# Turning the values of a gated delta rule: blocks on VectorE and a pass through DRAM in place of TensorE transposes

## The chip, the cores and the metric

The kernel runs on one core of one Trainium2 chip. The metric is device time in microseconds (us) of one execution; a kernel's time is the median of its runs.

## The reference

The reference is one inference step of a decoder layer with two parallel branches, a gated delta rule (A) and an indexer-sparse attention (B), for one prompt of 256 tokens and eight sequences of eight new tokens each. One wide input projection feeds both branches. Of branch A this matters here:

```python
h = rms_norm(x, pre_norm_g) * (1.0 + scale[:, None]) + shift[:, None]
(a_qkv, a_z, a_b, a_a, b_q, ...) = split_columns(h @ w_in)
...
qkv, conv_new = causal_short_conv(a_qkv, conv_buf, conv_w)
q, k, v = jnp.split(qkv, [A_QK, 2 * A_QK], axis=-1)
...
v = v.reshape(B, L, GDN_V_HEADS, GDN_DV)
...
o, s = gated_delta_rule(q, k, v, g, beta, s0)
```

There are 16 heads of q and k and 32 of v, all 128 wide. The delta rule needs each value head with tokens along one axis and the head's 128 channels along the other, while the projection delivers it with channels on the partitions.

## The kernel before, in words

All of the layer's large products are one stream on TensorE (`stream`). It takes blocks of 128 output columns of a weight matrix; each block is two units, one for each half of the 2048 input rows. A unit is 24 matmuls of 128x320 (256 prompt tokens and 64 new ones): weights are split in two parts (`whi` by ScalarE, `wlo` by VectorE as the difference), and the unit multiplies `whi` with `xh` and `xl`, then `wlo` with `xh`. The raw weights come in tiles `raw`, three tiles of two halves, so six units' worth; a half is 512 KB in rows of 512 bytes. `split_ahead` splits two units ahead of the one that is multiplied. The results of a block lie in a PSUM bank `pm`.

The recurrent stage (`gdn_chunks`) runs through eight groups of two q/k heads and four value heads. A group's blocks are k, q, z and v heads in this order. When a block is done, its function (`k_done`, `q_done`, `z_done`, `v_done`) takes it through a short convolution (`conv`); a value head ends in `vf`, a tile of 128 channels by 384 columns: 256 of the prompt, then for each sequence eight of the keys' and eight of the queries' places. After every second value head, `v_then` starts four generators for that pair of heads, h:

- `v_gen` turns the pair's values into `vt`, of 128 tokens by 3 blocks of tokens by 2 heads by 128 channels, and scales each token;
- `prompt_chain` and `sample_chain` do the recurrence, with `vt` and with `XT`, the inverse of a triangular matrix;
- `norm_gen` normalises, turns back and multiplies with z.

The inverse (`inverse`) is made once for a group, by GpSimd on 32x32 blocks; it stores `BT` to DRAM as 32x32 blocks (`d_b`), loads them as `blk`, and returns the result through `d_x`. Both chains wait for it and for `vt`.

The order on every engine is fixed when the program is built. The generators are advanced by `side_round`, twice in each unit. A planner, `Clock`, keeps an estimated time for each engine and for the DMA engines; a generator that yields a time is not advanced before TensorE's estimated time has reached it. For a transfer, `enter` charges each row with at least 512 bytes at 320 GB/s, and takes it to have landed 2.2 us after that. So a change of these costs moves instructions, though it changes none of them.

Nearly all transfers are issued by SyncE's queue in this fixed order: the weights, the states `S`, the buffers `cst` of the convolution, `gbt` with the decays, the stores of results. An issue stands at the head until what it waits for is there. `stream` and the planner issue a weight load when its half-tile is free, by the planner's time.

In `v_gen` before, each pair of heads takes two PSUM banks `ps`, `p` and `q`. TensorE turns the two heads' three blocks of 128 tokens in six 128x128 transposes (`self.tr`, a matmul with the identity `ident`), and ScalarE copies them to `vt` in three scalings by `sst`:

```python
for t in range(2):
    self.tr(p[:, 256 * t + 128 * v:256 * t + 128 * v + 128], vf[:, 128 * t:128 * t + 128])
self.tr(q[:, 128 * v:128 * v + 128], vf[:, 256:384])
```

There are two tiles `vt` and three `vf`. `vt` is free again when both chains of its pair are done.

Of the kernel before, what the change touches and what calls it, by code (L numbers as in the profile page):

```python
# [7 lines left out]
F32 = mybir.dt.float32  # L8
# [3 lines left out]
AF = mybir.ActivationFunctionType  # L12
# [38 lines left out]
class Engine:  # L51


    def __init__(self, engine, name, enter):
        self.engine, self.name, self.enter = engine, name, enter
# [11 lines left out]
class Engines:  # L67
    def __init__(self, nc, enter):
        for name in ("tensor", "vector", "scalar", "gpsimd", "sync"):
            setattr(self, name, Engine(getattr(nc, name), name, enter))  # L70


class Clock:
# [79 lines left out]
    def enter(self, name, op, args, kw):  # L153
        out = args[0] if args else kw["out"]
        rest = list(args[1:]) + list(kw.values())
        ins = [a for a in rest if hasattr(a, "tensor") and a is not out and a is not kw.get("accum_out")]
        outs = [out] + ([kw["accum_out"]] if kw.get("accum_out") is not None else [])
        if op == "transpose":
            ins = ins[:1]
        own = None if "dma" in op else name  # L160
        start = max(self.t[name], self.ready(*ins, name=own))
        if "dma" not in op or out.space != MEM.DRAM:
            start = max(start, self.idle(*outs, name=own))
        if name in ("vector", "scalar"):
            banks = {a.tensor.name for a in outs + ins if a.space == MEM.PSUM}
            for b in banks:
                start = max([start] + [t for e, t in self.bank.get(b, {}).items() if e != name])
        if "dma" in op:
            side = out if out.space != MEM.DRAM else ins[0]
            rows = self.free(side) // min(out.shape[-1], ins[0].shape[-1])  # L170
            size = side.shape[0] * rows * max(512, 4 * min(out.shape[-1], ins[0].shape[-1]))
            self.t[name] = start + (1.0 if name == "gpsimd" else 0.55)
            self.t["dma"] = max(self.t["dma"], start) + size / 3.2e5
            end = max(self.t["dma"], start) + 2.2
        else:
            if kw.get("op") == OP.pow or OP.pow in rest:
                took = 1.6
            else:
                took = self.cost(name, op, outs, ins)
            end = self.t[name] = start + took  # L180
            end += 0.2 if name == "tensor" else 0.1
        if name in ("vector", "scalar"):
            for b in banks:
                self.bank.setdefault(b, {})[name] = end
        by = "dma" if "dma" in op else name
        for a in ins:
            self.note(self.used, a, by, end)
        for a in outs:
            self.note(self.written, a, by, end)
        self.last = max(self.last, end)  # L190
# [11 lines left out]
class Kernel:  # L202
# [209 lines left out]
    def build(self):  # L412
        nc, tc = self.nc, self.tc
# [4 lines left out]
        f = self.fix  # L418
# [11 lines left out]
        self.d_z = self.dram.tile([32, 128, NT], F32, name="d_z")  # L430
        self.d_yb = self.dram.tile([KB, 128, NT], F32, name="d_yb")
        self.d_g = self.dram.tile([32, 384], F32, name="d_g")
        self.d_qi, self.d_q = (self.dram.tile([NB, 32, 4, 128], F32, name=n) for n in ("d_qi", "d_q"))
        self.d_b = [self.dram.tile([4, 12, 32, 32], F32, name=f"d_b{j}") for j in range(2)]
        self.d_x = [self.dram.tile([2, 4, 12, 32, 32], F32, name=f"d_x{j}") for j in range(2)]
# [2 lines left out]
        c = self.open("gdnc")  # L438
# [1553 lines left out]

    def v_gen(self, h, G):

        e, hv, K = h % 2, 2 * h, self.K[h]
        while "ready" not in G:
            yield
        yield self.ready(self.V[hv], self.V[hv + 1], G["sst"])
        yield from self.need(self.vt)
        yield from self.need(self.ps_side, 2)  # L2000
        vt = self.vt.get()
        p, q = self.psum(), self.psum()
        for v in range(2):
            vf = self.V.pop(hv + v)
            for t in range(2):
                self.tr(p[:, 256 * t + 128 * v:256 * t + 128 * v + 128], vf[:, 128 * t:128 * t + 128])
            self.tr(q[:, 128 * v:128 * v + 128], vf[:, 256:384])
            self.vf.put(vf)
        for t in range(3):
            src = p[:, 256 * t:256 * t + 256] if t < 2 else q[:, 0:256]  # L2010
            self.act(vt[:, t], src.rearrange("p (v d) -> p v d", v=2), AF.Copy,
                     scale=G["sst"][:, 20 + 3 * e + t:21 + 3 * e + t])
        self.ps_side.put(p)
        self.ps_side.put(q)
        K["vt"], K["users"] = vt, 2

    def drop_vt(self, K):
# [421 lines left out]
```

## Time and profile before

| What | us |
|---|---|
| Median of 3 runs | 2153.73 (2153.57 to 2154.71) |
| The profiled execution | 2151.39 |
| Its span, from the first to the last instruction | 2149.6 |
| TensorE matmuls busy | 2122.4 |
| VectorE busy | 1402.6 |
| ScalarE busy | 991.3 |
| GpSimd busy | 462.3 |

The profile is of one execution. Names stand without their buffer numbers: `ps<-ident,vf` is a matmul that writes a bank `ps` from `ident` and `vf`. PE is TensorE's matmuls and PEld its loads of weights, which overlap them; DVE is VectorE, ACT ScalarE, POOL GpSimd, SPq the queue of SyncE. In a group of instructions the figures are the busy time of all, the mean of one in ns, and the idle time of the engine just before them with what ended it. Nearly all instructions carry one line number, that of a helper that records them, so that groups are told apart by their tiles. The stage of the recurrence lies from about 730 to 1670 us; the value turns lie between 800 and 1560 us.

### The profile page before, as it was taken

What the parts mean: (1) busy time and instruction counts of PE and PEld (TensorE: products, weight loads), DVE (VectorE), ACT (ScalarE), POOL (GpSimd) and SP (SyncE); (2) the same over time, 40 slices, a digit from 0 to 9 for tenths busy, and PEclk for the clock granted to TensorE, in tenths of its full rate; (3) what the DMA queues carried; (4) which work ended last, traced back from release to release, by engine and by line L of the source; (5) the groups of instructions that cost most, each with busy time, mean ns of one, the idle gap of its engine ahead of it and who ended that gap; (6) DMA issues with size and microseconds to landing.
All of it is one profiled execution on the core that took longest, in us unless ns stands there. A gap on an engine that the chain in (4) does not pass through costs nothing.

```text
span 2149.6 us, 44001 instructions
## 1 busy us (share of the span) xinstructions
PE 2122.4 (99%) x17087; PEld 2028.8 (94%) x17087; DVE 1402.6 (65%) x2864; ACT 991.3 (46%) x2257; POOL 462.3 (22%) x645
## 2 busy tenths in 40 slices
PE   7999999999999999999999999999999999999997
PEld 6889999999999999899999999999999999999997
DVE  4665555889754577877777777777746645445443
ACT  3225465333343455465656565656545424323343
POOL 1001000000011018353535353536350000000000
PEclk9999999999999999999999999999999999999999
DMA  9995555985688766777777777777786967555562
GB/s 336 356 293 154 164 159 150 288 260 153 183 245 246 204 179 177 203 199 207 200 204 209 196 204 200 211 192 197 197 233 199 273 186 214 160 157 144 164 181 87
DMA packets 720336, 438.91 MB, mean 204 GB/s; under 512 B 74144, under 2 KB 705536, under 8 KB 717824
## 3 DMA queue, kind: packets, MB, share of 16 engines
q1 hardware_dynamic: 716032, 413.45, 68.2%
q0 software_dynamic: 3616, 21.02, 2.9%
q8 instruction: 134, 2.20, 0.4%
q10 hardware_dynamic: 480, 1.65, 0.2%
q14 instruction: 74, 0.61, 0.1%
HBM read 386.81 MB, written 48.94 MB: 203 GB/s over the span
## 4 chain that ended last, share of the span: by engine, by line
PE 71%; issue 23%; DMA 2%; DVE 2%; ACT 1%; SPq 0%; DVEq 0%; POOL 0%; POOLq 0%
PE pm L61 55%; PE ps L61 16%; DMA raw<-in_w_ada_dram 1%; DVE S L61 1%; DMA a<-in_w_ada_dram 1%; DVE ps L61 0%; DVE wlo L61 0%; SPq L61 0%; DMA c<-in_c_sample_dram 0%; DMA out_dram<-S 0%; ACT ot L61 0%; DMA cst<-in_state_conv_dram 0%; DVE w L61 0%; ACT whi L61 0%; DVE sc L61 0%
## 5 line engine op out<-in xcount | busy, mean ns | idle before, releaser
L61 PE MATMUL pm<-xh,whi 128*128 128x320 f32 x3284 | 1005.7, 319 | 0.6 <-ACT whi L61 0.3
L61 PE MATMUL pm<-xl,whi 128*128 128x320 f32 x3284 | 971.9, 309 | 0.3 <-DVE xl L61 0.3
L61 DVE TENSOR_TENSOR wlo<-raw,whi 128x1024 fp32r<-128x1024 f32 x474 | 587.4, 1248 | 291.7 <-ACT whi L61 270.3
L61 PEld LDWEIGHTS pm<-xh,whi 128*128 128x128 f32 x3284 | 617.1, 188 | 30.6 <-issue 24.4
L61 PEld LDWEIGHTS pm<-xl,whi 128*128 128x128 f32 x3284 | 617.6, 188 | 1.7 <-DVE xl L61 0.8
L61 ACT ACTIVATE whi<-raw 128x1024 fp32r<-128x1024 f32 x474 | 498.1, 1058 | 163.2 <-PE pm L61 149.9
L61 PE MATMUL pm<-xh,wlo 128*128 128x320 f32 x3284 | 553.3, 309 | 0.0
L61 PEld LDWEIGHTS pm<-xh,wlo 128*128 128x128 f32 x3284 | 499.3, 188 | 0.0
L61 POOL TENSOR_TENSOR X<-X,tmpx 48x31 f32<-48x31 f32 (+15 forms) x248 | 175.2, 706 | 19.4
L61 POOL TENSOR_TENSOR tmpx<-blk,X 48x31 f32<-48x31 f32 (+15 forms) x248 | 162.0, 653 | 52.1 <-DMA blk<-d_b 34.0
L61 PE MATMUL pm<-y1h,whi 128*128 128x320 f32 x512 | 151.3, 309 | 1.0 <-ACT y1h L61 1.0
L61 PE MATMUL pm<-y1l,whi 128*128 128x320 f32 x512 | 151.2, 308 | 0.1
L61 DVE SCALAR_TENSOR_TENSOR ps<-xp,cs,ps 128x344 f32<-128x344 f32 x192 | 111.5, 581 | 6.8
L61 POOL TENSOR_TENSOR rfin<-rfin,mh 128x3 f32<-128x3 f32 x1 | 0.8, 848 | 485.9 <-DVE rfin L61 485.9
L61 POOL TENSOR_TENSOR sc<-sc,mh 128x6 f32<-128x6 f32 (+1 forms) x24 | 43.5, 1814 | 280.7 <-DVE sc L61 253.8
L61 PEld LDWEIGHTS pm<-y1h,whi 128*128 128x128 f32 x512 | 96.2, 188 | 1.3 <-ACT y1h L61 1.3
L61 PEld LDWEIGHTS pm<-y1l,whi 128*128 128x128 f32 x512 | 95.9, 187 | 0.3 <-DVE y1l L61 0.3
L61 PE MATMUL pm<-y1h,wlo 128*128 128x320 f32 x512 | 85.4, 308 | 0.0
L61 PEld LDWEIGHTS pm<-y1h,wlo 128*128 128x128 f32 x512 | 77.7, 188 | 0.0
L61 DVE SCALAR_TENSOR_TENSOR S<-S,gtr,ps 128x128 f32<-128x128 f32 x256 | 67.5, 342 | 0.1
L61 ACT ACTIVATE xp<-pm 128x256 f32<-128x256 f32 (+1 forms) x128 | 32.0, 304 | 71.1 <-PE pm L61 71.1
L61 ACT ACTIVATE ot<-ot,sc 128x128 f32<-128x128 f32 x96 | 29.9, 390 | 71.8 <-DVE sc L61 71.8
(372 smaller groups left out, 2319.8 us busy)
## 6 DMA issues: line engine op xcount, KB each, us to landing
raw<-in_w_in_dram SPq DMA_DIRECT2D x336, 512.0 KB
raw<-in_w_pa_dram SPq DMA_DIRECT2D x64, 512.0 KB
rawx<-in_w_ada_dram SPq DMA_DIRECT2D x18, 1024.0 KB
a<-in_w_ada_dram SPq DMA_DIRECT2D x16, 1024.0 KB
S<-in_state_gdn_dram SPq DMA_DIRECT2D x32, 512.0 KB
out_dram<-S SPq DMA_DIRECT2D x32, 512.0 KB
raw<-in_w_pb_dram SPq DMA_DIRECT2D x32, 512.0 KB
raw<-in_w_out_dram SPq DMA_DIRECT2D x32, 512.0 KB
```

What stands on the lines that cost most here:

```text
L61: made = fn(*args, **kw)
```

## The change

`v_gen` no longer uses TensorE or PSUM. It takes `vt` as soon as a tile is free, without waiting for the scale factors `sst`. VectorE transposes each head's `vf` in blocks of 32x32 straight into half of `vt` (`nc.vector.transpose` on 128x384), which leaves every block turned within its own place but the blocks themselves in channel order. Eight transfers then store `vt` to a new DRAM tensor `d_v` of 384 tokens by 2 heads by 128 channels, one for each head and each group of 32 channels; each writes rows of 32 numbers, 128 bytes, to their token's place. A ninth transfer loads `d_v` into the same `vt`, now in token order, in rows of 1 KB. ScalarE scales `vt` in place, when the load is there and the factors are.

Beside that, the planner charges a transfer's row with at least 256 bytes instead of 512, for all transfers of the kernel.

```diff
-            size = side.shape[0] * rows * max(512, 4 * min(out.shape[-1], ins[0].shape[-1]))
+            size = side.shape[0] * rows * max(256, 4 * min(out.shape[-1], ins[0].shape[-1]))
...
+        self.d_v = [self.dram.tile([384, 2, 128], F32, name=f"d_v{j}") for j in range(2)]
...
     def v_gen(self, h, G):
 
+        nc = self.nc
         e, hv, K = h % 2, 2 * h, self.K[h]
+        yield self.ready(self.V[hv], self.V[hv + 1])
+        yield from self.need(self.vt)
+        vt = self.vt.get()
+        yield self.idle(vt)
+        blocks = vt.rearrange("p t v d -> p (t v d)")
+        for v in range(2):
+            vf = self.V.pop(hv + v)
+            self.emitted += 1
+            nc.vector.transpose(blocks[:, 384 * v:384 * v + 384], vf)
+            self.vf.put(vf)
+        yield
+        d = self.d_v[e]
+        for v in range(2):
+            for i in range(4):
+                src = blocks[32 * i:32 * i + 32, 384 * v:384 * v + 384]
+                nc.sync.dma_start(d[:, v, 32 * i:32 * i + 32].rearrange("(n r) c -> r n c", r=32),
+                                  src.rearrange("r (n c) -> r n c", c=32))
+        yield max(self.ready(d), self.idle(vt))
+        nc.sync.dma_start(vt, d.rearrange("(t p) v c -> p t v c", t=3))
         while "ready" not in G:
             yield
-        yield self.ready(self.V[hv], self.V[hv + 1], G["sst"])
-        yield from self.need(self.vt)
-        yield from self.need(self.ps_side, 2)
-        vt = self.vt.get()
-        p, q = self.psum(), self.psum()
-        for v in range(2):
-            vf = self.V.pop(hv + v)
-            for t in range(2):
-                self.tr(p[:, 256 * t + 128 * v:256 * t + 128 * v + 128], vf[:, 128 * t:128 * t + 128])
-            self.tr(q[:, 128 * v:128 * v + 128], vf[:, 256:384])
-            self.vf.put(vf)
+        yield self.ready(vt, G["sst"])
         for t in range(3):
-            src = p[:, 256 * t:256 * t + 256] if t < 2 else q[:, 0:256]
-            self.act(vt[:, t], src.rearrange("p (v d) -> p v d", v=2), AF.Copy,
-                     scale=G["sst"][:, 20 + 3 * e + t:21 + 3 * e + t])
-        self.ps_side.put(p)
-        self.ps_side.put(q)
+            self.act(vt[:, t], vt[:, t], AF.Copy, scale=G["sst"][:, 20 + 3 * e + t:21 + 3 * e + t])
         K["vt"], K["users"] = vt, 2
```

What it moves is seen in the lists of instructions as they stand in the two programs. On TensorE, at the first pair of value heads, before: the end of one unit (`whi`, then eight `wlo`), the six turns into the banks ps_69 and ps_70, and the next unit's first matmul.

```order
L61 MATMUL pm_66<-xh,whi_78 128x320
L61 MATMUL pm_66<-xl,whi_78 128x320
L61 MATMUL pm_66<-xh,wlo_81 128x320 x8
L61 MATMUL ps_69<-ident,vf_7336 128x128 x2
L61 MATMUL ps_70<-ident,vf_7336 128x128
L61 MATMUL ps_69<-ident,vf_7337 128x128 x2
L61 MATMUL ps_70<-ident,vf_7337 128x128
L61 MATMUL pm_65<-xh,whi_79 128x320
```

The same place now:

```order
L61 MATMUL pm_66<-xh,whi_78 128x320
L61 MATMUL pm_66<-xl,whi_78 128x320
L61 MATMUL pm_66<-xh,wlo_81 128x320 x8
L61 MATMUL pm_65<-xh,whi_79 128x320
L61 MATMUL pm_65<-xl,whi_79 128x320
```

The units follow each other directly. Over the whole program TensorE has 96 matmuls fewer and none more; some of the chains' pieces stand a little earlier or later among the units.

On SyncE's queue, where the third group begins, before: weight loads (raw), the recurrent states S, a result w, two z tiles zf and the decays gbt.

```order
L61 DMA out_dram<-w_7359 128x2x128
L61 DMA S_7366<-in_state_gdn_dram 128x8x128 x2
L61 DMA out_dram<-S_7367 128x8x128 x2
L61 DMA raw_75<-in_w_in_dram 128x8x128
L61 DMA out_dram<-w_7361 128x2x128
L61 DMA zf_7342<-d_z 128x320
L61 DMA zf_7340<-d_z 128x320
L61 DMA raw_75<-in_w_in_dram 128x8x128
L61 DMA gbt_7343<-d_g 128x768
L61 DMA raw_76<-in_w_in_dram 128x8x128
```

And now, at the place that answers to it:

```order
L61 DMA S_7368<-in_state_gdn_dram 128x8x128 x2
L61 DMA out_dram<-w_7363 128x2x128
L61 DMA out_dram<-S_7369 128x8x128 x2
L61 DMA raw_75<-in_w_in_dram 128x8x128
L61 DMA d_v_90<-vt_7357 32x12x32 x8
L61 DMA raw_75<-in_w_in_dram 128x8x128
L61 DMA zf_7344<-d_z 128x320
L61 DMA zf_7343<-d_z 128x320
L61 DMA gbt_7345<-d_g 128x768
L61 DMA raw_76<-in_w_in_dram 128x8x128
L61 DMA vt_7357<-d_v_90 128x3x256
```

The eight stores stand between two weight loads, and the load of `vt` comes two weight loads later. It is much the same at most of the other pairs.

On the same queue one group earlier, at the first pair of the second group, before:

```order
L61 DMA raw_77<-in_w_in_dram 128x8x128 x2
L61 DMA blk<-d_b_93 48x1024
L61 DMA raw_75<-in_w_in_dram 128x8x128
L61 DMA out_dram<-S_7366 128x8x128 x2
L61 DMA raw_75<-in_w_in_dram 128x8x128
L61 DMA out_dram<-w_7358 128x2x128
L61 DMA S_7366<-in_state_gdn_dram 128x8x128 x2
L61 DMA out_dram<-S_7367 128x8x128 x2
L61 DMA raw_76<-in_w_in_dram 128x8x128
L61 DMA cst_104<-in_state_conv_dram 24x256
```

And now:

```order
L61 DMA raw_75<-in_w_in_dram 128x8x128 x2
L61 DMA blk<-d_b_95 48x1024
L61 DMA out_dram<-S_7368 128x8x128 x2
L61 DMA S_7368<-in_state_gdn_dram 128x8x128 x2
L61 DMA out_dram<-w_7360 128x2x128
L61 DMA out_dram<-S_7369 128x8x128 x2
L61 DMA out_dram<-w_7363 128x2x128
L61 DMA d_v_90<-vt_7357 32x12x32 x8
L61 DMA cst_106<-in_state_conv_dram 24x256
```

Before, weight loads stand between the stores and loads of states. Now there is none from `blk` on, nor behind the last row: three more loads of `cst`, two of `S`, eight stores `out_dram<-cst` and one load of `gbt` follow before the next `raw`. These are 32 issues in a row; nowhere else in the stage are there so many.

## Prediction

> **What bounds the kernel now.** I read the page's head first: which engine is full, and over what span.
>
> ```profile
> span 2149.6 us, 44001 instructions
> PE 2122.4 (99%) x17087; PEld 2028.8 (94%) x17087; DVE 1402.6 (65%) x2864; ACT 991.3 (46%) x2257; POOL 462.3 (22%) x645
> ```
>
> TensorE is busy nearly all the time, but that is an average over stages, so the table of stretches comes next. Its columns are the busy time of PE, PEld, DVE, ACT and POOL with counts in brackets, then the granted clock, the busy share of the 16 DMA engines and GB/s.
>
> ```profile
> 0.00:700.00 700.00, 688.77 (x6002) 632.77 (x6002) 458.25 (x916) 274.96 (x540) 44.17 (x68) 1.00 0.77 230
> 700.00:1700.00 1000.00, 996.47 (x8093) 959.61 (x8092) 728.67 (x1673) 555.22 (x1483) 417.28 (x576) 1.00 0.75 203
> 1700.00:2150.00 450.00, 437.16 (x2996) 436.46 (x2994) 215.69 (x276) 161.13 (x234) 0.85 (x1) 0.99 0.57 166
> ```
>
> The recurrent stage lies in the second row. There TensorE is idle for 3.5 us of 1000, at a clock of 1.00; DVE has a quarter of the time free, ACT almost half, the DMA engines a quarter. What ends TensorE's waits is in the list of waits, cut to 800 to 1560 us, in which the value turns lie:
>
> ```profile
> PE ps L61 <- DVE S L61: 1.1, 2, 0.6
> PE ps L61 <- DMA cst<-in_state_conv_dram: 0.9, 1, 0.9
> PE pm L61 <- ACT whi L61: 0.3, 1, 0.3
> ```
>
> That is 2.3 us in 760: no other engine or transfer holds TensorE. An instruction taken from its queue here shortens the run by its own slot, as long as nothing new makes it wait. In the third row TensorE is full for 437 of 450 us as well, so the gain should survive to the end.
>
> **What TensorE is relieved of.** The change removes 96 transposes (16 pairs of value heads, six each) and adds nothing to TensorE's list. Three views price them. First the groups by line of the stage, one row for the turns and one for the weight loads that belong to them:
>
> ```profile
> L61 PE MATMUL ps<-ident,vf 128*128 128x128 f32 x96 | 13.4, 274 | 1.1 <-DVE S L61 1.1
> L61 PEld LDWEIGHTS ps<-ident,vf 128*128 128x128 f32 x96 | 11.1, 141 | 1.6 <-DVE S L61 1.6
> ```
>
> Then the chain of work around one such group, with start, length and count (pm is the projection, ps everything else):
>
> ```profile
> 1109.69 0.88 PE ps L61 x6
> 1110.57 1.77 PE pm L61 x12
> 1112.34 0.66 PE ps L61 x6
> 1112.99 10.56 PE pm L61 x72
> ```
>
> The six turns at 1112.34 take 0.66 us of the chain, 0.11 us each, and the projection goes on at its usual 10.56/72 = 0.147 us. So 16 x 0.66 = 10.6 us is the lower bound, and the 13.4 us in which any of them was in flight the upper; the weight loads' 11.1 us lie between. I take 11.5 us, near the chain and the loads, plus a little for the change of operand. The mean of 274 ns is no price, since neighbours overlap. The Trainium skill (TensorE: Matmul & The Clock Gate, Part 4: PE-mode transpose) gives about 275 ns for a 128x128 transpose within a kernel; the duration agrees (274 ns), but by it the sum would be an estimate of 96 x 0.275 = 26.4 us, over twice what the chain shows.
>
> **What VectorE and ScalarE get.** VectorE gets 32 block transposes of 128x384. The same operation stands in the trace at another size, and ScalarE's old scaling beside one of its copies from SBUF:
>
> ```profile
> L61 DVE STREAM_TRANSPOSE a<-a 128x1024 f32<-128x1024 f32 x24 | 28.8, 1227 | 0.0
> L61 ACT ACTIVATE vt<-ps,sc 128x256 f32<-128x256 f32 x48 | 18.9, 462 | 5.9 <-PE ps L61 5.9
> L61 ACT ACTIVATE ot<-ot,sc 128x128 f32<-128x128 f32 x96 | 29.9, 390 | 71.8 <-DVE sc L61 71.8
> ```
>
> In proportion, 384/1024 x 1.23 = 0.46 us each; at most 0.6 with a fixed part. That is 15 to 19 us over the stage, on an engine with 1000 - 729 = 271 us free: covered. What waits behind a pair of turns are the next subtraction of weights and the next convolution, by about 1 us, and the split weights are made two units ahead (24 matmuls x 0.147 = 3.5 us each). ScalarE keeps its 48 scalings; reading SBUF in place of PSUM moves them by tenths of a microsecond either way. Both cost the end nothing.
>
> **What the DMA engines get.** Per pair: eight stores of 384 packets of 128 bytes, and one load of 0.39 MB. The inverse's stores d_b<-BT have exactly the stores' shape. In the DMA view of 787 to 791 us, which holds little else, the busiest queue's row gives packets, MB and share of 16 engines:
>
> ```profile
> q1 hardware_dynamic: 1976, 0.29, 45.5%
> ```
>
> 0.455 x 4 us x 16 / 1976 = 14.7 ns per small packet. All 49,152 take 49,152 x 14.7 / 16 = 45 us. The loads move 6.3 MB, at 203/0.75 = 271 GB/s another 23 us. On 0.75 x 760 = 570 us this makes 638 us, a share of 0.84. It fits, and nobody on TensorE waits for it.
>
> **What the queue of issues gets.** SyncE issues nearly every transfer, in order, the weights (raw) among them; 9 issues a pair are added, 144 in all. The rows: what d_b's stores took in a quiet and in a crowded place, one load that follows such stores (shortest, median, longest), and SyncE's largest wait between 800 and 1560 us:
>
> ```profile
> 787.02 2.02 SPq L61 DMA_DIRECT2D d_b<-BT  x4
> 872.26 4.61 SPq L61 DMA_DIRECT2D d_b<-BT  x4
> L61 SPq DMA_DIRECT2D blk<-d_b x8: 455/1306/1496, 794.1 to 1528.7; - x8
> SPq L61 <- DVE wlo L61: 164.8, 69, 10.4
> ```
>
> A store takes 0.5 to 1.15 us, so a burst of eight 4.0 to 9.2 us, the load 0.5 to 1.5 us; 72 to 171 us over the stage. SyncE stood with a weight load in hand, waiting for its buffer, for 165 us there. That slack carries the addition, at the upper end barely. A load delayed by one burst hurts no one: six half-tiles are in the ring, 6 x 3.5 = 21 us of projection, and a burst is at most 10.7.
>
> One place differs: where the order shows 32 issues between two weight loads. The same kinds of issue, from the time line:
>
> ```profile
> 893.53 2.07 SPq L61 DMA_DIRECT2D out_dram<-S  x2
> 897.79 0.95 SPq L61 DMA_DIRECT2D out_dram<-w  x1
> 898.86 2.13 SPq L61 DMA_DIRECT2D S<-in_state_gdn_dram  x2
> 902.06 2.83 SPq L61 DMA_DIRECT2D out_dram<-S  x2
> 908.61 0.35 SPq L61 DMA_DIRECT2D gbt<-d_g  x1
> 910.37 3.19 SPq L61 DMA_DIRECT2D S<-in_state_gdn_dram  x2
> 917.29 3.98 SPq L61 DMA_DIRECT2D out_dram<-cst  x8
> ```
>
> With w twice these add to 16.5 us for 18 issues; five more small ones at 0.3 to 0.5 make 18.5, and the eight stores 22.5 to 27.7 us, against a ring of 21 and two split units, 7 us, behind it. TensorE may wait 0 to 6.5 us there, once. I take 1.5, since the low end is covered twice.
>
> **The waits that the change adds.** A pair's values come later by a round trip through DRAM. The row of the turns and that of their first use, with first and last start:
>
> ```profile
> L61 PE MATMUL ps<-ident,vf x96: 271/273/328, 801.0 to 1559.9; 128*128 128x128 f32 x96
> L61 PE MATMUL ps<-vt,XT x192: 270/275/347, 875.9 to 1634.7; 128*128 128x128 f32 x192
> ```
>
> Some 75 us lie between, because the chains wait for the inverse. A round trip of 10 to 20 us is hidden. ScalarE's scaling now waits for the load, and behind it stand the roundings of weights (whi); the program puts it after the time at which its planner takes the load to be there, so it costs nothing if that is right. The smaller floor for rows in the planner changes only when instructions are put into the queues.
>
> **The sum.** -11.5 (bounds -10.6 to -13.4) + 1.5 (0 to 6.5) = -10.0 us. The profiled execution took 2151.4 us, 1.8 more than its span, and the median of the runs is 2153.7; the sum gives 2141.4 for the one and 2143.7 for the other. A difference of 0.2%, 4.3 us, is about what a measurement of this kernel can tell from none.
>
> **Rivals.** *Half is given back.* SyncE's slack is eaten by stores at the crowded price, 1.15 us, and each pair makes TensorE wait 0.5 us for weights: 16 x 0.5 = 8 us, 2150.2. For it: 171 us of issue against 165 us of slack. Against it: only loads later than ring and split together, 28 us, reach TensorE.
>
> *Slower: ScalarE stands at the load.* The same pattern, stores and a load of what they wrote, made GpSimd wait in this trace (total, times, longest):
>
> ```profile
> POOL tmpx L61 <- DMA blk<-d_b: 34.0, 2, 21.6
> ```
>
> If ScalarE is held so, the roundings behind it are late, and it decides from 7 us on, the lead of two units. Waits of 21.6 and 12.4 us at two of the sixteen pairs would give 14.6 + 5.4 = 20 us, net +8.5: 2162.2. Against it: the load of gbt, put by the same rule, has no row among VectorE's waits.
>
> *Slower: the small packets are dear.* If each 128-byte write cost as two 512-byte packets, the stores would be 50 MB, at 271 GB/s 186 us; with 570 and 23 the engines would need 779 us where TensorE, its 11.5 us saved, needs 748.5: 30.5 us more than 2142.2, so 2172.7. The 14.7 ns above speak against it. The Trainium skill (DMA: Bandwidth & Descriptors, Specifications) has such a rule: below 512 bytes a DMA engine does a read-modify-write. The row of 787 us, writes of 128 bytes among its packets, shows no such price.
>
> **How the numbers follow.** Forecast 0.72, half given back 0.12, ScalarE held 0.11, dear packets 0.02, the full 13.4 us and the 1.1 us wait of the turns beside it gone too (2139.2) 0.03. Predicted is 2143.7. The range runs from that 2139.2 to 2152.0: the upper end takes in the forecast's worst (2153.7 - 10.6 + 6.5 = 2149.6) and half given back with a little more; beyond it lie the two slower rivals. Faster by over 0.2% means below 2149.4: the forecast, the full gain and a part of the second rival, 0.78. Within 0.2%: the rest of that rival and the forecast's end, 0.09. Slower: 0.13.
>
> **What would show it.** TensorE's stage row with 3 to 6 us idle in 1000 and 96 fewer matmuls; block transposes of 0.46 to 0.6 us; DMA share near 0.84; no wait of ScalarE for a load of d_v above 7 us. A large row of whi waiting for raw, or of PE waiting for whi, would make the first or second rival right; a share near 1.0 with TensorE idle, the third.

## The result and the profile after: 0.8% slower

| | before | after |
|---|---|---|
| median of 6 runs each, side by side (lowest to highest) | 2152.69 us (2150.52 to 2154.71) | 2169.76 us (2167.40 to 2173.58) |
| ratio, 95% interval | | 1.0083 (1.0073 to 1.0093) |
| profiled execution, its span | 2151.4 us, 2149.6 us | 2167.4 us, 2165.7 us |

The forecast was 2143.7 us, range 2139.2 to 2152.0. The head of the page after, 96 matmuls fewer and the engines hardly busier:

```profile
span 2165.7 us, 44037 instructions
PE 2123.0 (98%) x16991; PEld 2025.9 (94%) x16991; DVE 1425.1 (66%) x2896; ACT 994.2 (46%) x2257; POOL 467.2 (22%) x645
```

The recurrent stage in the table of stretches, columns as in the prediction:

```profile
700.00:1700.00 1000.00, 981.59 (x7908) 941.39 (x7906) 741.62 (x1691) 550.11 (x1472) 422.16 (x576) 0.99 0.81 212
```

TensorE's idle time there went from 3.5 to 18.4 us, and its clock is no longer 1.00. The DMA share is 0.81, far from full. What ended TensorE's waits from 800 to 1560 us, the stretch shown of before (total, times, longest):

```profile
PE ps L61 <- DMA cst<-in_state_conv_dram: 6.3, 3, 2.4
PE ps L61 <- DMA cst<-in_conv_w_dram: 4.2, 2, 2.6
PE pm L61 <- ACT whi L61: 2.0, 2, 1.3
```

The first two rows add up to 10.5 us, where 0.9 stood before. cst is the tile into which the convolution's state and weights of the next group are loaded (`conv_gen`, four small loads by SyncE); TensorE turns it. The turns and the scaling, by line of the stage, and the stores and the load of the pass in the view of tile d_v (shortest, median and longest issue in ns):

```profile
L61 ACT ACTIVATE vt<-vt,sc 128x256 f32<-128x256 f32 x48 | 20.9, 500 | 7.0 <-DMA vt<-d_v 4.5 <-issue 1.8 <-DMA raw<-in_w_in_dram 0.6
L61 DVE STREAM_TRANSPOSE vt<-vf 128x384 f32<-128x384 f32 x32 | 16.4, 547 | 0.0
```

```profile
L61 SPq DMA_DIRECT2D d_v<-vt x128: 302/480/3258, 807.2 to 1591.8; - x128
L61 SPq DMA_DIRECT2D vt<-d_v x16: 367/1020/2556, 815.8 to 1599.8; - x16
```

These came as forecast: 547 ns a turn, 0.48 us a store, ScalarE held for the load by 4.5 us in all and not by 34.

**One of the waits.** SyncE's time line in the third group:

```profile
1015.75 4.51 SPq L61 DMA_DIRECT2D d_v<-vt  x8
1020.36 1.06 SPq L61 DMA_DIRECT2D raw<-in_w_in_dram  x2
1021.47 1.04 SPq L61 DMA_DIRECT2D gbt<-d_g  x1
1022.73 0.37 SPq L61 DMA_DIRECT2D vt<-d_v  x1
1023.15 0.46 SPq L61 DMA_DIRECT2D cst<-in_state_conv_dram  x1
1023.65 0.29 SPq L61 DMA_DIRECT2D cst<-in_conv_w_dram  x1
```

and TensorE's, with the idle time before the matmul and its releaser in brackets:

```profile
1026.28 1.33 PE L61 MATMUL pm<-xh,wlo 128*128 128x320 f32 x8
1030.04 0.35 PE L61 MATMUL ps<-ident,cst 92*128 92x92 f32 x2 [2.42 <-DMA cst<-in_state_conv_dram]
```

The load of the values, 0.39 MB, is issued directly ahead of the small loads of cst. TensorE comes to the transposes of cst at 1027.6, 4.5 us after the first issue; it can start them 6.9 us after it. At four of the five waits for cst (1027, 1141, 1249 and 1360 us) the load of the values stands 0.4 to 0.7 us ahead in this way, and cst is used 6.9 to 8.8 us after its issue. At the fifth (1050 us) it does not, and TensorE comes only 2.7 us after the issue. Behind none of the other loads of cst in that stretch does TensorE wait. In before the same group's two sets of loads, each with a weight load (raw, 0.5 MB) 0.4 to 0.5 us ahead, were used 4.8 and 7.2 us after their first issue without a wait; SyncE's lines and TensorE's:

```profile
1017.78 0.38 SPq L61 DMA_DIRECT2D raw<-in_w_in_dram  x1
1018.21 0.55 SPq L61 DMA_DIRECT2D cst<-in_state_conv_dram  x1
...
1024.32 0.39 SPq L61 DMA_DIRECT2D raw<-in_w_in_dram  x1
1024.80 1.59 SPq L61 DMA_DIRECT2D cst<-in_state_conv_dram  x1
```

```profile
1023.00 0.32 PE L61 MATMUL ps<-ident,cst 92*128 92x92 f32 x2
...
1031.99 0.32 PE L61 MATMUL ps<-ident,cst 92*128 92x92 f32 x2
```

So it is not any large load directly ahead that makes cst late. The load of the values does, as far as the four places show it; why it delays cst more than a weight load does stays open.

In after, the stretch of the wait and 3.4 us soon behind it, in the table of stretches:

```profile
1026.00:1030.00 4.00, 1.62 (x12) 1.35 (x10) 1.86 (x4) 2.10 (x7) 3.69 (x5) 1.00 1.09 314
```

```profile
1031.13:1034.54 3.41, 3.41 (x16) 3.41 (x15) 3.35 (x10) 3.08 (x8) 3.17 (x4) 0.51 0.91 238
```

The DMA engines are full (share 1.09) while cst is waited for. Then the clock granted to TensorE falls to half for 3.4 us. The projection's matmuls start 0.27 us apart there (1031.58, 1031.84, 1032.11) and not 0.147, which costs about 1.5 us. Up to 1710 us this follows four times, on idle times of 1.9 to 2.6 us (1027, 1249, 1360 and 1698 us): some 6 us. Idle times of 1.6 and 1.7 us in the same trace (1050 and 1141 us) are not followed by it. In before no idle time of the stage is longer than 1.0 us and the clock stays at 1.00. The Trainium skill (TensorE: Matmul & The Clock Gate, Part 1: The HAM clock gate) has such a window of 3413 ns and half clock after an idle one; the length agrees, but here less than a whole idle window was enough.

**The account.** Taking the distance from each weight load's start to the next against the median that the same two neighbours have in before, the new instruction list is 10.8 us shorter (the forecast's 11.5). Distances that exceed that by over 0.5 us rise from 3.9 to 21.1 us in the stage, +17.2; smaller excesses rise in the stage by 6.9 us and in the part after 1700 us by 1.6 us, the halved clock among them. That makes +14.9 of the 16.1 us by which the span grew. Of the waits in the stage, cst has 9.6 us more than before and all others together some 5 us more. How the few pairs of neighbours that before does not have are priced moves the 10.8 us by about half a microsecond.

### The profile page after: what moved, and what is told of

Its sections match the earlier page's. It is cut to its first block, busy times and chain, and to the rows that moved or that the text cites. A ratio compares the mean times of both kernels' runs of the same rounds, so it can differ in the third digit from the quotient of the medians.

```text
span 2165.7 us, 44037 instructions
## 1 busy us (share of the span) xinstructions
PE 2123.0 (98%) x16991; PEld 2025.9 (94%) x16991; DVE 1425.1 (66%) x2896; ACT 994.2 (46%) x2257; POOL 467.2 (22%) x645
## 4 chain that ended last, share of the span: by engine, by line
PE 63%; issue 23%; DVE 5%; DMA 5%; SPq 2%; ACT 1%; DVEq 0%; POOL 0%; POOLq 0%; ACTq 0%
PE pm L61 48%; PE ps L61 15%; SPq L61 2%; DVE S L61 2%; DMA raw<-in_w_ada_dram 1%; DVE wlo L61 1%; DVE ps L61 1%; DMA a<-in_w_ada_dram 1%; DMA cst<-in_state_conv_dram 1%; DMA d_v<-vt 1%; DMA vt<-d_v 0%; DMA cst<-in_conv_w_dram 0%; ACT ot L61 0%; ACT ps L61 0%; DVE w L61 0%
```

## The experiments

Medians of 4 to 11 runs, ratios to the kernel before run beside them. "Idle" is 1000 less TensorE's busy time from 700 to 1700 us in the table of stretches.

| kernel | what it is | us | ratio (95%) | idle, us |
|---|---|---|---|---|
| before | | 2152.7 | 1 | 3.5 |
| after | pass, turns moved, floor 256 | 2169.8 | 1.0083 (1.0073 to 1.0093) | 18.4 |
| e2 | before, floor 256 | 2151.0 | 0.9995 (0.9986 to 1.0004) | 2.3 |
| e1 | after, floor 512 | 2153.7 | 1.0008 (0.9999 to 1.0017) | 9.2 |
| e12 | after, only d_v charged at 512 | 2150.0 | 0.9991 (0.9982 to 1.0000) | 6.7 |
| e18 | after, only d_v charged at 1024 | 2179.6 | 1.0127 (1.0111 to 1.0142) | 21.8 |
| e3 | after, cst's transposes held 6 us | 2164.2 | 1.0065 (1.0051 to 1.0079) | 18.5 |
| e19 | after, cst counted 2.5 us later | 2170.3 | 1.0084 (1.0070 to 1.0098) | 20.8 |
| e7 | after, cst loaded by ScalarE | 2159.7 | 1.0038 (1.0025 to 1.0052) | 14.7 |
| e6, e13 | before plus the pass, floor 256 / 512 | 2177.1, 2176.7 | 1.0120 (1.0104 to 1.0135), both | 15.9, 14.8 |
| e5, e8 | after without the pass, floor 256 / 512 | 2161.9, 2160.8 | 1.0048 (1.0034 to 1.0062), 1.0041 (1.0027 to 1.0055) | 16.9, 16.0 |
| e14 | before without the turns | 2161.1 | 1.0050 (1.0036 to 1.0063) | 16.3 |
| e20 | as e14, in the order of before | 2157.2 | 1.0024 (1.0014 to 1.0034) | 14.3 |
| e21 | whole change, in the order of before | 2186.3 | 1.0165 (1.0151 to 1.0179) | 30.5 |
| e9 | e1, stores two at a time | 2156.0 | 1.0018 (1.0009 to 1.0027) | 11.5 |
| e10 | e1, pass issued by GpSimd | 2238.4 | 1.0406 (1.0392 to 1.0421) | 52.7 |
| e16 | e1, second group turned by TensorE | 2154.6 | 1.0011 (1.0002 to 1.0020) | 9.8 |
| e17 | e12, second group's pass 30 us later | 2149.9 | 0.9991 (0.9982 to 1.0000) | 6.6 |

The ranges written down before each run stand below in full. In e1, e7, e10, e18 and e21 the time fell into none of them; in e12, e17 and e19 it missed the nearest by 1 us or less.

### Floor and pass (e1, e2, e12, e18)

The first question was whether the planner's smaller floor or the pass itself makes cst late. e1, the whole change with the old floor:

```diff
-            size = side.shape[0] * rows * max(256, 4 * min(out.shape[-1], ins[0].shape[-1]))
+            size = side.shape[0] * rows * max(512, 4 * min(out.shape[-1], ins[0].shape[-1]))
```

> The change with the planner's floor put back to 512 bytes a row; the pass through DRAM stays. Theory A (SyncE's nine added transfers a pair make the loads of cst land late, and TensorE stands at their transposes; its clock then falls for 3.4 us after each long wait): the pass is still there, so 2163 to 2172 us, TensorE waits for cst of 8 us or more. Theory B (the lower floor makes the planner count on loads too early, and that alone brings the waits): 2140 to 2147 us, waits for cst below 2 us. Theory C (the small packets take bandwidth from the weights): 2163 to 2172 us, with waits for whi or raw instead of cst.

e2, the kernel before with the floor of 256 alone:

> The kernel before with one number changed, the planner's floor of 256 bytes a row; TensorE turns the values, no pass. Theory B1 (the lower floor by itself makes in-order engines stand at loads): it costs here what putting it back has won in the change, some 14 to 16 us: 2160 to 2168 us, waits of TensorE for cst. Theory B2 (the lower floor hurts only together with the pass's nine transfers, which make loads late): 2150 to 2155 us, waits as in the kernel before.

e2 shows no loss: the floor alone costs nothing in the kernel before. With the floor at 512 the change costs 16 us less than at 256 (2153.7), and no wait for cst is left. e12 puts 512 back for the transfers of d_v only:

```diff
-            size = side.shape[0] * rows * max(256, 4 * min(out.shape[-1], ins[0].shape[-1]))
+            size = side.shape[0] * rows * max(512 if "d_v" in out.tensor.name + ins[0].tensor.name else 256, 4 * min(out.shape[-1], ins[0].shape[-1]))
```

> The changed kernel, with the floor of 256 for every transfer but those of d_v, which the planner charges at 512 again. Theory E (the planner counts the pass's eight stores at half, so the loads of the convolution's state behind them are counted on 2.5 us too early and TensorE stands at the transposes of cst): like the kernel with the floor of 512 everywhere, 2151 to 2157 us, TensorE's waits for cst 0 to 1 us. Rival F (the smaller floor acts through the other transfers, those of the inverse or the stores of the outputs): as the changed kernel, 2166 to 2172 us, waits for cst some 10 us.

2150.0 us: one number of the planner, for one kind of transfer, is worth 19.8 us. Its row of the stage, and SyncE's time line at the place shown of after:

```profile
700.00:1700.00 1000.00, 993.33 (x8028) 953.97 (x8027) 751.18 (x1709) 558.21 (x1487) 423.12 (x576) 1.00 0.82 217
```

```profile
1015.72 4.19 SPq L61 DMA_DIRECT2D d_v<-vt  x8
...
1022.20 0.39 SPq L61 DMA_DIRECT2D cst<-in_state_conv_dram  x1
...
1033.98 0.39 SPq L61 DMA_DIRECT2D vt<-d_v  x1
```

and TensorE's time line of e12:

```profile
1029.18 0.32 PE L61 MATMUL ps<-ident,cst 92*128 92x92 f32 x2
```

The burst stands where it stood, but the load of the values is now issued 11 us behind the loads of cst and not 0.4 us ahead of them, and TensorE comes to cst 7.0 us after the issue and finds it there. At the three groups that follow it comes 5.5 to 6.6 us after the issue and does not wait, where after needed 7.6 to 8.8. So cst is there sooner in this order. The DMA engines are just as full here (share 1.14 from 1022 to 1029 us), so full engines alone do not make TensorE wait. By the planner's line eight stores take 32 x 12 x 256 bytes x 8 / 3.2e5 = 2.5 us with the floor of 256 and 4.9 us with 512; with the smaller charge it takes the round trip for done sooner, and the load is issued before cst.

e18 charges d_v at 1024. If reserve were all that counts, it would be as good as e12:

> The changed kernel with the transfers of d_v charged at 1024 and the others at 256. Theory E (the planner must count the pass at no less than it takes; more reserve costs nothing): 2147 to 2153 us with no wait for cst. Rival H (the order is what counts and any new charge shuffles it): 2155 to 2168 us with waits of TensorE for another engine or load.

It is slower than e12 by 30 us, and TensorE waits for another engine, from 800 to 1560 us:

```profile
PE pm L61 <- ACT whi L61: 16.6, 9, 3.3
```

So the charge does not act as a reserve alone: it selects an order, and each order has its own waits.

### Is it the cst loads? (e3, e19, e7)

e3 holds TensorE's transposes of cst back by 6 us behind the planned landing, the charge stays:

```diff
-            yield
+            yield self.clock.last + 6.0
             yield from self.need(self.ps_side)
             p = self.psum()
             for k in range(2):
                 self.tr(p[:, 128 * k:128 * k + 92], t[0:92, 128 * k:128 * (k + 1)])
```

> The change with one edit: the transposes of cst are put into TensorE's queue 6 us later by the planner's time, loads unmoved. Theory A: the waits for cst and the dips of the clock behind them go, some 15 us in all; what is left of the waits is for weights and states: 2144 to 2153 us. Theory B: the same, since it also acts through these waits. Theory C: the weights stay late, 2163 to 2172 us.

e19 counts only the landing of cst later:

```diff
-            end = max(self.t["dma"], start) + 2.2
+            end = max(self.t["dma"], start) + (4.7 if out.tensor.name.startswith("cst") else 2.2)
```

> The changed kernel, floor and pass as they are, but the planner counts the loads of cst alone as landing 2.5 us later (4.7 us after their slot in place of 2.2). Theory E (TensorE's transposes of cst are put into its queue before the loads can be there): TensorE's waits for cst 0 to 2 us in place of 10.5, no halved clock from them, and 2148 to 2157 us. Rival F (the charge of 512 helped by moving other transfers, not by cst): waits for cst gone but others in their place, 2160 to 2170 us.

e7 takes the loads of cst off SyncE's queue:

```diff
-                nc.sync.dma_start(t[r:r + 24, :], sc[:, c0:c0 + 256])
-                nc.sync.dma_start(t[r + 24:r + 28, :], cw[:, c0:c0 + 256])
+                nc.scalar.dma_start(t[r:r + 24, :], sc[:, c0:c0 + 256])
+                nc.scalar.dma_start(t[r + 24:r + 28, :], cw[:, c0:c0 + 256])
```

> The changed kernel with the four loads of cst issued by ScalarE in place of SyncE, so that they do not stand behind the pass's stores. Theory E: no wait for cst; ScalarE gives four issues a half group, and if these cost it nothing the time is 2148 to 2157 us. Rival I (the loads are late because the DMA engines are full of the pass's packets, whatever queue issues them): waits for cst stay at 8 to 12 us and the time at 2164 to 2172 us.

In all three the waits for cst are gone or under 1 us, so they do come from transposes that stand too early in TensorE's list for these loads: in the third group TensorE comes to them 10.1 us after the first issue in e3, 7.6 and 9.5 us after it in e7. In e7, then, it is also TensorE's later coming that ends the waits, and not only the other queue. But e19 gets nothing back, e3 5.6 us and e7 10. What stands in e19's waits instead (800 to 1560 us):

```profile
PE pm L61 <- ACT whi L61: 9.3, 5, 6.0
PE pm L61 <- DVE wlo L61: 7.6, 8, 1.8
```

and in e7's, TensorE's first and ScalarE's for the load:

```profile
PE pm L61 <- DVE wlo L61: 6.5, 5, 2.0
```

```profile
ACT vt L61 <- DMA vt<-d_v: 16.9, 6, 4.4
```

The theory that cst alone is the cause falls: cst is where this order waits, and the orders without those waits have others.

### Does the saving arrive at all? (e5, e8, e14, e20)

e5 leaves out the stores and the load of the pass (the values stay in block order), e8 does the same with the floor of 512:

```diff
-        d = self.d_v[e]
...
-        yield max(self.ready(d), self.idle(vt))
-        nc.sync.dma_start(vt, d.rearrange("(t p) v c -> p t v c", t=3))
```

> The change without the pass through DRAM: VectorE's block transposes and ScalarE's scaling stay, the eight stores and the load are left out, so values stay in block order. Theory A: TensorE's 10.8 us are saved and nothing is given back: 2140 to 2146 us. Theory B: the lower floor is still there, waits for cst stay: 2150 to 2165 us. Theory C: as A, 2140 to 2146 us.

> The change without the pass through DRAM, and with the floor at 512 bytes; values stay in block order. Theory B1: TensorE's 10.8 us and nothing against it, 2140 to 2145 us. Rival D (VectorE's 17 us of block transposes make the scalings and the split weights late, whatever the floor): waits for whi and wlo stay as in the run without the pass at 256, 2155 to 2162 us.

e14 is the kernel before without any turn (the values are scaled unturned, in six pieces):

```diff
-            for t in range(2):
-                self.tr(p[:, 256 * t + 128 * v:256 * t + 128 * v + 128], vf[:, 128 * t:128 * t + 128])
-            self.tr(q[:, 128 * v:128 * v + 128], vf[:, 256:384])
+            for t in range(3):
+                self.act(vt[:, t, v], vf[:, 128 * t:128 * t + 128], AF.Copy,
+                         scale=G["sst"][:, 20 + 3 * e + t:21 + 3 * e + t])
```

> The kernel before with the six turns of a pair left out: ScalarE scales the values unturned in six pieces in place of three, nothing is added to VectorE, SyncE or the DMA engines, the floor stays 512 (the values are not turned). Theory G (TensorE's saving arrives wherever nothing new makes it wait): 11 us less than before, 2139 to 2144 us. Rival H (any change of the list makes the planner lay out another order, and that one has waits of its own worth 8 to 20 us): 2149 to 2162 us, with waits of TensorE for whi, wlo or cst of 5 us or more in the stage.

All three have 96 transposes less and no pass, and all three are 9 to 10 us slower than before. TensorE's list is 11 us shorter in each by the account above, but its idle time is 12 to 14 us longer, and the clock was halved twice in each. e14 has no block transposes on VectorE and loses as much, so these are not needed for the loss. Each removal also made the planner lay out another order. e20 excludes that: it leaves the turns out as e14 does, but tells the planner of them, so that every other instruction stands in the order of before on every engine:

```diff
+    def plan_tr(self, out, in_):
+        self.pe_ns += 110
+        self.emitted += 1
+        self.clock.enter("tensor", "transpose", (out, in_, self.ident), {})
...
-                self.tr(p[:, 256 * t + 128 * v:256 * t + 128 * v + 128], vf[:, 128 * t:128 * t + 128])
-            self.tr(q[:, 128 * v:128 * v + 128], vf[:, 256:384])
+                self.plan_tr(p[:, 256 * t + 128 * v:256 * t + 128 * v + 128], vf[:, 128 * t:128 * t + 128])
+            self.plan_tr(q[:, 128 * v:128 * v + 128], vf[:, 256:384])
```

> The kernel before with the turns left out as in e14 (ScalarE scales the values unturned, in six pieces), but the planner is told of the six turns and three scalings as before, so every other instruction stands in the order of before on every engine. Theory H (the order that the planner lays out anew costs what TensorE saves): 2139 to 2145 us, 16 to 22 us less than e14 with the same work. Rival J (the work left out is what makes the following engines late, since TensorE runs ahead of them): 2152 to 2162 us, as e14.

2157.2 us, 4 us less than e14 but 5 more than before, outside the range of the theory that only the order costs. But e20 does not only leave out: ScalarE's six pieces are work that before did not have. e20's waits of TensorE from 800 to 1560 us have one row of weight:

```profile
PE pm L61 <- ACT whi L61: 12.0, 13, 1.6
```

It is 13 waits of about 0.9 us; 12 of them end with the first rounding behind a pair's six pieces. ScalarE's time line of before at one of these places, and TensorE's:

```profile
1024.10 1.87 ACT L61 ACTIVATE ot<-ot,sc 128x128 f32<-128x128 f32 x6 [5.03 <-DVE sc L61]
1025.87 0.25 ACT L61 ACTIVATE cst<-ps 128x128 f32<-128x128 f32 x1
1026.03 1.18 ACT L61 ACTIVATE vt<-ps,sc 128x256 f32<-128x256 f32 x3
1027.09 1.06 ACT L61 ACTIVATE whi<-raw 128x1024 fp32r<-128x1024 f32 x1
```

```profile
1028.47 0.31 PE L61 MATMUL pm<-xh,whi 128*128 128x320 f32 x1
```

The same in e20:

```profile
1025.39 1.87 ACT L61 ACTIVATE ot<-ot,sc 128x128 f32<-128x128 f32 x6 [5.05 <-DVE sc L61]
1027.17 0.26 ACT L61 ACTIVATE cst<-ps 128x128 f32<-128x128 f32 x1
1027.32 1.85 ACT L2018 ACTIVATE vt<-vf,sc 128x128 f32<-128x128 f32 x6
1029.08 1.04 ACT L61 ACTIVATE whi<-raw 128x1024 fp32r<-128x1024 f32 x1
```

```profile
1030.17 0.41 PE L61 MATMUL pm<-xh,whi 128*128 128x320 f32 x1 [0.91 <-ACT whi L61]
```

In before ScalarE stands 5.0 us until VectorE has the row scales (sc), scales the outputs, scales the values, and rounds the next weights: ready at 1028.15, used by TensorE at 1028.47. The lead is 0.3 us, not the two units (7 us) that the prediction took. It is 0.1 to 0.4 us behind ten of the 16 pairs' scalings, 1.4 us behind one, and 2.4 to 4.9 us behind the other five. Counted from the start of the output scaling (ot), TensorE comes to the unit 4.37 us later in before and 3.87 us in e20 (1030.17 less its wait), 0.50 us earlier, and the six pieces take 0.67 us longer than the three: 0.50 + 0.67 - 0.32 = 0.85 us of wait, and 0.91 was measured. So the larger part of e20's waits is its own pieces. Without them the wait would be about 0.2 us, and e20 some 8 us faster (12 x 0.67), about 2149 us, between the two theories; that is an estimate from these rows, no run shows it.

In the changed kernel the scalings stand elsewhere. The first rounding behind them is ready 2.3 us or more ahead of its use at 14 of the 16 pairs in after and 1.7 us or more at all 16 in e12, and TensorE waits behind none of them. So this short lead is not what slows the changed kernel.

### The pass (e6, e13, e21, e9, e10)

e6 adds the nine transfers of a pair to the kernel before, behind its scaling, with the floor of 256; e13 does it with 512. TensorE still turns (the values come back with their blocks permuted):

```diff
             self.act(vt[:, t], src.rearrange("p (v d) -> p v d", v=2), AF.Copy,
                      scale=G["sst"][:, 20 + 3 * e + t:21 + 3 * e + t])
+        yield
+        nc, d = self.nc, self.d_v[e]
...
+        yield max(self.ready(d), self.idle(vt))
+        nc.sync.dma_start(vt, d.rearrange("(t p) v c -> p t v c", t=3))
+        yield self.ready(vt)
```

> The kernel before, TensorE's turns kept, with the nine transfers of the pass added behind the scaling and with the floor of 256 bytes; the pass changes the order of the values' blocks. Theory A: all of the price and nothing of the gain, 2152.7 + 17 to 28 = 2170 to 2181 us, with waits of TensorE for cst. Theory B: some of it, 2155 to 2170 us, and the same without the pass. Theory C: 2170 to 2181 us, waits for whi or raw.

> The kernel before with the nine transfers added after its scaling and the floor left at 512; TensorE and ScalarE turn and scale as before (the values come back with their blocks permuted). Theory E (floor and pass together make the cst loads late): no wait for cst and 2152 to 2158 us, against 2177 with the floor of 256. Rival F (nine more transfers a pair cost that much by themselves, however they are charged): 2170 to 2180 us. TensorE keeps its 96 turns in both, so nothing is saved.

Both cost 25 us, with different waits: e6 waits 10.6 us for cst, e13 shares its wait among whi, X (the inverse as it is loaded back from d_x), cst and others. So the floor is not what decides in every order; with the pass alone, 512 does not help. e21 lays the whole change into the order of before, unseen by the planner (stores 9, load 18, scalings 30 us behind the old turns):

```diff
+            raw.vector.engine.transpose(blocks[:, 384 * v:384 * v + 384], vf)
...
+        at = self.clock.t["tensor"]
+        yield at + 9.0
...
+                raw.sync.engine.dma_start(d[:, v, 32 * i:32 * i + 32].rearrange("(n r) c -> r n c", r=32),
+                                          src.rearrange("r (n c) -> r n c", c=32))
+        yield at + 18.0
+        raw.sync.engine.dma_start(vt, d.rearrange("(t p) v c -> p t v c", t=3))
+        yield at + 30.0
```

> The whole change (turns by VectorE, eight stores and a load through DRAM, scaling after it), but laid into the order of before: the planner counts the old turns and scalings and does not know of the new instructions, the stores are put 9 us, the load 18 us and the scalings 30 us behind the place of the old turns. Every other instruction stands as before. Theory H (the order, not the work, makes the change slower): 2140 to 2148 us, as the forecast had it, with TensorE's waits in the stage below 8 us. Rival J (the pass's nine issues and transfers cost 10 us or more in any order): 2154 to 2170 us, with waits for loads that stand behind the pass.

2186.3 us, the slowest but e10 and outside both ranges: 34 us more than before. TensorE's waits from 800 to 1560 us:

```profile
PE ps L61 <- DMA cst<-in_conv_w_dram: 22.0, 6, 5.4
PE pm L61 <- ACT whi L61: 2.0, 2, 1.1
```

and SyncE's time line at the group that waits 2.8 us at 1035:

```profile
1026.97 4.85 SPq L2034 DMA_DIRECT2D d_v<-vt  x8
...
1033.99 0.55 SPq L61 DMA_DIRECT2D cst<-in_state_conv_dram  x1
```

A burst put ahead of the cst loads without moving their transposes makes TensorE stand there six times, once for each group loaded in that stretch. So the order of before has no room for the pass at these places, and with the planner's new orders it costs less: 34 us more than before in the old order, 17 in the changed kernel, none in e12. Other places in the old order were not tried.

e9 issues the stores two at a time (a `yield 0.0` behind every second one), e10 puts all nine transfers on GpSimd's queue (`nc.gpsimd` for `nc.sync`), both with the floor of 512:

> The change with the floor at 512 bytes and the eight stores of a pair issued two at a time, a half unit apart, so that weight loads come between them. If the rest of the loss at 512 comes from bursts of stores ahead of weights in SyncE's queue: 2143 to 2149 us. If from the transfers themselves or from the order of the chains: 2151 to 2156 us, as with the burst.

> The change with the floor at 512 bytes and the pass's nine transfers issued by GpSimd instead of SyncE. If SyncE's queue is what delays weights and states: 2142 to 2149 us. If the packets on the DMA engines are: 2151 to 2158 us. GpSimd's inverse is slowed by its issues, some 9 us a pair, which the chains have room for.

Spreading changes little (2156.0 against e1's 2153.7). GpSimd is the wrong queue: the groups by line of e10's page, and TensorE's waits from 800 to 1700 us:

```profile
L61 POOL DMA_DIRECT2D d_v<-vt x128 | 79.2, 626 | 0.5 <-issue 0.4
```

```profile
PE pm L61 <- ACT whi L61: 38.4, 9, 8.4
```

The issues occupy the engine that works on the inverse for 79 us, and TensorE loses 38 us to late weights. How one leads to the other was not followed further.

### The second group (e16, e17)

What TensorE still waits in e1 lies mostly from 890 to 955 us. e16 turns the two pairs of the second group on TensorE again (`if h in (2, 3)` the old code); e17 is e12 with `yield self.clock.last + 30.0` ahead of that group's stores:

> The changed kernel with the floor of 512, and the two pairs of the second group turned by TensorE as before, the other fourteen by VectorE and DRAM. Theory E: the steady groups are clean with the floor of 512 and what it loses lies in the second group, where SyncE's queue is crowded, so 14/16 of the saving of 11.5 us is left, minus 0 to 3 us at the end of the stage: 2141 to 2146 us. Rival H (another plan, other waits): 2149 to 2160 us.

> The kernel with only the pass charged at 512 (2150.0 us), and the stores of the second group's two pairs held back by some 30 us, out of the stretch of 890 to 950 us in which SyncE's queue is crowded. Theory E (what is left lies in that stretch, 6 us of waits there): 2143 to 2147 us. Rival H (another order, other waits): 2150 to 2160 us.

e16 gains nothing on e1; e17's waits in that stretch for the weights shrink from e12's three of 0.6 to 2.0 us to one of 0.8, but a wait of 0.8 us comes at 1357 and a halved clock at 902 us: 2149.9 us, as e12. e12 and e17 are the best versions: 1.9 to 2.1 us less than the kernel before run beside them, at the edge of what can be told from no change.

## Why the prediction was wrong, point by point

- **"A load delayed by one burst hurts no one": wrong, and the step that failed in the changed kernel.** It was worked out for the weights, which have a ring of 21 us, and put everything else at nothing. SyncE also loads cst, straight onto TensorE's path, and in before TensorE comes to it 5 to 8 us after the issue. In after it came 2.7 to 6.2 us after it at five places, at four of them with the load of the values directly ahead of cst, and waited 10.5 us; three of the four halved clocks came from there too. This is the largest term of the loss.
- **"Nobody on TensorE waits for it": wrong for the same reason.** The DMA share was 0.81 (0.84 forecast) and the small packets were cheap, so the third rival did not come. But it is not the share that decides: at the place shown the engines are full both in after, which waits, and in e12, which does not.
- **"The smaller floor for rows in the planner changes only when instructions are put into the queues": true, and given no term in the sum.** That is the whole effect of the floor. 256, 512 and 1024 for the same transfers gave 2169.8, 2150.0 and 2179.6 us.
- **TensorE's saving: right in size.** -11.5 was forecast; by the account the list is 10.8 us shorter in after and about 11 in e12. "An instruction taken from its queue here shortens the run by its own slot, as long as nothing new makes it wait": in no run was the saving left whole. In after the condition failed, as cst shows. In e5, e8 and e14, which have no pass, the planner's new order brought other waits. e20 kept the order, but added work to ScalarE. No run takes out the turns and nothing else.
- **The cover of ScalarE: wrong for before, unharmed in after.** "The split weights are made two units ahead" does not hold behind ten of the old scalings: 0.1 to 0.4 us were left. At the place shown the wait for sc took the rest, one of those in the 71.8 us of the prediction's own row of ot. In the changed kernel the scalings moved to places with more lead. ScalarE's scaling did not wait long for the load (4.5 us in all), as forecast, so the second rival did not come.
- **The crowded stretch: right in size.** 1.5 us (0 to 6.5) was forecast; TensorE waits 2.5 us for weights from 890 to 960 us in after and 3.5 us in e12. The sum there counts 19 issues, not 18, and 27.7 less 21 is 6.7 us, not 6.5; neither changes the forecast.
- **VectorE: right.** 547 ns a turn against 460 to 600.
- **Not thought of:** the halved clock, some 6 us.
- **The rival "half given back"** had its place (SyncE's queue) but not its price or its victim: it counted weights.

Forecast for the profiled execution: -10.0; its span grew by 16.1. In e12, with one charge put back, the span of the profiled execution, its fastest, is 4.1 us shorter than that of before, and the median 1.9 us. What stays open is why the pass alone costs 25 us at either floor, why the load of the values delays cst as it does, and whether any order of this planner keeps all of the 11 us; the runs show none.

## What to carry to other kernels

A busy share of 99% does not tell how close other work is to making that engine wait: where a planner has laid everything just in time, look for each engine's lead at the place of the edit (ready time to use time in the time line), not for its idle time over the stage. When transfers are added to a queue, list every load behind them with its own lead, the small ones for TensorE first. And where a change touches a planner's costs, run it with two or three values of that cost before judging the change: here the spread between them, 30 us, is almost three times the saving.

## What the runs showed of the hardware that was not expected

- The clock granted to TensorE fell to half for 3.4 us on four idle times of 1.9 to 2.6 us in the changed kernel; such an idle time cost about 1.5 us more than it lasted. The runs show no fixed threshold: in e14 an idle time of 2.95 us (1038 us) was not followed by it, and in e17 one came at 902 us though no idle time near it was longer than 1.2 us.
- Four small loads (two of 24 KB, two of 4 KB) were used 6.9 to 8.8 us after their first issue, with a wait, at four places where the load of the values (0.39 MB, from a tensor stored just before) had been issued 0.4 to 0.7 us ahead of them on the same queue. Behind a weight load of 0.5 MB in before, 4.8 us were enough. What makes the difference is open.
- 49,152 stores of 128-byte packets and 6.3 MB of loads raised the stage's DMA share only from 0.75 to 0.81, and to 0.82 in e12, close to the 0.84 that 14.7 ns for each packet had given.
